# One layer of a hybrid streaming encoder on one core: the output projection's gate summed on VectorE, inverse roots as exp of a logarithm, capped decay differences as Relu

## The chip, the core and the metric

The kernel runs on one core of one Trainium2 chip. The core has five engines with a queue each: PE (TensorE, matmuls), DVE (VectorE), ACT (ScalarE), POOL (GpSimd) and SP (SyncE, which here only issues DMAs). The metric is the device time of one execution in microseconds (us).

## What is computed

One layer for two request groups that share the weights, 256 prompt tokens and 32 sample tokens (together T = 288 columns; 128 features to a partition tile, NB = 16 tiles for 2048). Everything is in fp32. Cut to what matters here:

```python
shift1, scale1, gate1, shift2, scale2, gate2 = split(silu(c) @ w_mod + b_mod, 6)
h = rms_norm(x) * (1 + scale1) + shift1
a, b, c_, gates = split(h @ w_in)
y_a = group_rms_norm(gla(a)) * silu(a_g)
y_b = group_rms_norm(ssd(b) * silu(z))
y_c = u * token_mix(layer_norm(v))
merged = sum_k sigmoid(g_k) * (y_k @ w_branch_k)
x = x + gate1 * (merged @ w_out)
x = x + gate2 * (square(relu(h2 @ w_up)) @ w_down)
```

The recurrence of branch B weighs pairs of positions with exp(min(a_t - a_s, 0)), masked to t >= s; the decay difference is capped at zero before the exp.

## The kernel before, in words

All large products go through `product_group`: a tile of 4 x 256 weight columns (512 KB) is loaded by SP into a ring of six `raw` buffers, ACT casts it to its high half (`whi`, line 443), DVE subtracts to get the low half (`wlo`, line 444), and PE runs 24 matmuls of 288 columns with them (lines 461 to 463: low activations with high weights, high with high, high with low). There are three buffers each of `whi` and `wlo`.

The modulation `silu(c) @ w_mod` has six parts of 2048 outputs. Parts 0 and 1 come first (`mod_stream`). The others follow in the order `MOD_PARTS = (2, 4, 3, 5)`; part 2 is `gate1`, the gate of the output projection. They are a generator, `mods`, that the product loops advance by fractions of a step for each weight tile (`mod_rate`, 0.2 to 0.5). One step is one 512 KB tile `mraw` of `w_mod`, in the same ring of six buffers.

Parts 4, 3 and 5 are summed on DVE (`mod_part_ve`, line 302): a unit is 512 columns, 8 steps; in each step four operations multiply a 128 x 512 piece by a column of `cT` and add it to one of two accumulators `macc` (lines 316 and 318). At the end eight small matmuls against `ones2` sum over partitions, ACT copies the result, PE transposes it once and DVE adds the bias (lines 372 to 385, called through `mod_flush`). Part 2 is summed on PE (`mod_parts`, lines 327 to 356): for each pair of tiles eight matmuls of 256 columns in four column groups, then per half of the part one copy on ACT and two transposes.

The mixers run beside the products. `mixer_c` normalises the eight tiles of v on DVE, transposes them on PE, and `finish_c` (line 1060) multiplies with `wsT` on PE, adds and multiplies on DVE (`yC`, `acc`); `split_y` makes `yhi` on ACT and `ylo` on DVE for the branch's products. `mixer_a` runs for eight heads; each builds `z` operands on DVE and ACT for seven levels, and ends with `inv_rms` (line 721): a matmul with `ones`, Sqrt on ACT, reciprocal on DVE. `mixer_b` (line 869) runs eight times; for each of two heads it forms the capped decay differences on DVE (line 923), takes Exp on ACT (lines 926 and 928) and multiplies with `cb` on DVE. After every fourth `mixer_b` and in `mixer_c` there is one more `inv_rms`.

What order the instructions have on each engine is decided when the kernel is built: a scheduler takes the ready instruction of the highest priority, program order with an offset for loads, weight halves and evacuations (`tc.high_priority`). On the chip every queue then runs in that order.

Of the kernel before, what the change touches and what calls it, by code (L numbers as in the profile page):

```python
# [10 lines left out]
F32 = mybir.dt.float32  # L11
# [6 lines left out]
P = 128  # L18
D = 2048
# [21 lines left out]
def tile_step(ctx, tc, io, outs):  # L41
# [12 lines left out]
    MOD_VE = (4, 3, 5)  # L54
# [6 lines left out]

    MODB = 2
# [264 lines left out]
    def mod_parts(parts):  # L327


        for part in parts:  # L330
            if part in MOD_VE:
                yield from mod_part_ve(part)
                continue
            for half in range(2):
                ps = paux.tile([P, 512], F32, tag="modps", name=nm("modps"), bufs=2)
                c0 = part * D + half * 1024
                held = []
                for k in range(NB):
                    with tc.high_priority(offset=PRIO):
                        raw = wpool.tile([P, 1024], F32, tag=MTAG[0], name=nm("mraw"), bufs=MTAG[1])  # L340
                        nc.sync.dma_start(out=raw, in_=wm[:, k, c0:c0 + 1024])
                    held.append((k, raw))
                    if len(held) == MODB:
                        together([partial(TE.matmul, ps[32 * cg:32 * cg + 32, 0:256], cT[:, k1, :],
                                          r[:, cg * 256:(cg + 1) * 256], start=k < MODB and k1 == k,
                                          stop=k == NB - 1 and k1 == held[0][0])
                                  for k1, r in reversed(held) for cg in range(4)])
                        held = []
                    if k == 1:
                        mod_flush()  # L350
                    yield
                with tc.high_priority(offset=PRIO):
                    sb = wpool.tile([P, 256], F32, tag="modsb", name=nm("modsb"), bufs=1)
                    S.copy(out=sb, in_=ps[:, 0:256])
                mod_tail.append((part * NB + half * 8, 0, ps, sb))
        mod_flush()

    mod_tail = []

    def mod_flush():  # L360

        while mod_tail:
            j, n, ps, sb = mod_tail.pop()
            if n:
                for b in range(n):
                    TE.matmul(ps[:, 2 * b:2 * b + 2], sb[:, b * P:(b + 1) * P], selm, start=True, stop=True)
                V.tensor_tensor(out=mod[:, j:j + n, :],
                                in0=ps[:, 0:2 * n].rearrange("p (b s) -> p b s", s=2),
                                in1=par("b_mod", j, n).unsqueeze(2).to_broadcast([P, n, 2]), op=ALU.add)
            else:  # L370
                nb = 2
                if type(sb) is list:
                    nb = 1
                    acc, sb = sb, wpool.tile([P, 256], F32, tag="modsb", name=nm("modsb"), bufs=1)
                    together([partial(TE.matmul, ps[32 * cg:32 * cg + 32, 0:P], ones2[:, s],
                                      acc[s][:, cg * P:(cg + 1) * P], start=s == 0, stop=s == 1)
                              for s in range(2) for cg in range(4)])
                    S.copy(out=sb[:, 0:P], in_=ps[:, 0:P])
                for b in range(nb):
                    TE.transpose(ps[:, b * P:(b + 1) * P], sb[:, b * P:(b + 1) * P], ident)  # L380
                v = ps[:, 0:nb * P].rearrange("p (b g r) -> p g b r", b=nb, r=32)
                m = mod[:, j:j + 4 * nb, :].rearrange("p (g b) s -> p g b s", b=nb)
                V.tensor_tensor(out=m, in0=v[:, :, :, 0:2], op=ALU.add,
                                in1=par("b_mod", j, 4 * nb).rearrange("p (g b) -> p g b", b=nb).unsqueeze(3)
                                .to_broadcast([P, 4, nb, 2]))
# [4 lines left out]
    mods = chain(mod_stream(boot), mod_parts(MOD_PARTS))  # L390
# [330 lines left out]
    def inv_rms(sq, scale):  # L721

        pq = aux()
        TE.matmul(pq[:, 0:T], ones, sq[:, 0:T], start=True, stop=True)
        r = tt("rms")
        S.activation(out=r[:, 0:T], in_=pq[:, 0:T], func=AF.Sqrt, scale=scale, bias=eps_c)
        V.reciprocal(out=r[:, 0:T], in_=r[:, 0:T])
        return r
# [140 lines left out]
    def mixer_b(j):  # L869
# [45 lines left out]
        for a in range(2):  # L915
# [5 lines left out]
            for o, rows, c, t0, n in ((m[:, 0:P], slice(0, P), 0, 0, P), (m[:, P:SEQ], slice(0, P), 1, P, P),  # L921
                                      (ms[LAST, a], LAST, 2, SEQ, DEC)):
                V.tensor_scalar(out=o, in0=pa[rows, t0:t0 + n], scalar1=tkm[rows, c, 1, hh:hh + 1], scalar2=0.0,
                                op0=ALU.subtract, op1=ALU.min)
            S.activation(out=e2[a * BP:(a + 1) * BP, 0:160], in_=pa[a * BP:(a + 1) * BP, 128:T], func=AF.Exp)
            S.activation(out=m[:, 0:SEQ], in_=m[:, 0:SEQ], func=AF.Exp)
            V.tensor_mul(out=m[:, 0:SEQ], in0=m[:, 0:SEQ], in1=cb[:, 0:SEQ])
        S.activation(out=ms[LAST], in_=ms[LAST], func=AF.Exp)
# [108 lines left out]
    def mixer_c():  # L1037
# [11 lines left out]
        rs = inv_rms(ss, 1.0 / 1024)  # L1049
# [286 lines left out]
```

## Time and profile before

| | us |
|---|---|
| median of 3 runs | 2059.65 (2055.81 to 2063.46) |
| the profiled execution | 2054.64 |
| its span, first to last instruction | 2052.9 |
| mean granted clock of PE in it | 0.993 of full speed |

The rows below come from the profiled execution; its times count from the start of the span. In a row of a group of instructions stand: line, engine, operation, output<-inputs, shapes, count, then busy time, mean ns of one, and the idle time of the engine before them with what ended it. PE's durations overlap, so starts are compared there.

### The profile page before, as it was taken

Reading aid. Unit: us, or ns where it says so; the run is one execution under the profiler, and the core shown is the slowest. Engines: PE = TensorE matmul, PEld = TensorE weight load, DVE = VectorE, ACT = ScalarE, POOL = GpSimd, SP = SyncE. Lnnn points to the kernel's source line nnn. Section 1 sums busy time; section 2 is a strip of 40 time slices with the busy share of each in tenths; the row PEclk is TensorE's granted clock in tenths of the full one; section 3 lists DMA queues with packets and bytes.
Section 4 is the critical chain, followed back from the end, with each engine's and each line's share of the span. In section 5 each row is a group of like instructions: output and inputs, shape, how many; then the busy total and the mean of one; then the engine's idle time right before and its main releaser. Section 6 shows DMA issues by size and latency. Waiting matters only on the chain.

```text
span 2052.9 us, 40220 instructions
## 1 busy us (share of the span) xinstructions
PE 2002.9 (98%) x16248; PEld 1941.6 (95%) x16248; DVE 1450.8 (71%) x2515; ACT 990.9 (48%) x1547; POOL 154.8 (8%) x284
## 2 busy tenths in 40 slices
PE   5999999999999999999999999999999999999997
PEld 3888999989999999999999999999999999999997
DVE  2585767866679878798889998675864455555564
ACT  3432595675555545555344544433443344334443
POOL 3020220100101101011000100000000000000010
PEclk8999999999999999999999999999999999999999
DMA  9998745556576766577777777575655555555542
GB/s 259 312 315 267 224 137 165 176 166 200 184 226 191 212 192 199 174 229 242 226 248 235 228 237 225 185 226 185 218 192 163 162 163 166 168 165 162 167 157 88
DMA packets 364874, 412.29 MB, mean 201 GB/s; under 512 B 14808, under 2 KB 325488, under 8 KB 364688
## 3 DMA queue, kind: packets, MB, share of 16 engines
q1 hardware_dynamic: 360784, 403.97, 63.2%
q0 software_dynamic: 3040, 4.58, 1.0%
q8 instruction: 127, 2.08, 0.4%
q10 hardware_dynamic: 864, 1.18, 0.2%
q14 instruction: 59, 0.48, 0.1%
HBM read 405.05 MB, written 4.62 MB: 200 GB/s over the span
## 4 chain that ended last, share of the span: by engine, by line
PE 61%; DVE 0%; ACT 0%; DMA 0%; issue 0%; DVEq 0%; ACTq 0%
PE mm L463 20%; PE mm L461 20%; PE mm L462 20%; DMA mraw<-in_w_mod_dram 0%; PE aux L1226 0%; PE aux L210 0%; ACT stage L1300 0%; PE aux L897 0%; PE modps L77 0%; PE modps L80 0%; PE aux L80 0%; PE aux L936 0%; DVE macc L318 0%; PE aux L885 0%; DVE wlo L444 0%
## 5 line engine op out<-in xcount | busy, mean ns | idle before, releaser
L443 ACT CAST whi<-raw 128x1024 fp32r<-128x1024 f32 x568 | 595.4, 1049 | 835.9 <-PE mm L462 652.8
L444 DVE TENSOR_TENSOR wlo<-raw,whi 128x1024 fp32r<-128x1024 f32 x568 | 695.2, 1225 | 410.5 <-ACT whi L443 408.8
L461 PE MATMUL mm<-hlo,whi 128*128 128x288 f32 x1408 | 419.8, 299 | 1.2 <-ACT sg L974 1.2
L462 PE MATMUL mm<-hhi,whi 128*128 128x288 f32 x1408 | 417.1, 297 | 0.0
L463 PE MATMUL mm<-hhi,wlo 128*128 128x288 f32 x1408 | 412.3, 297 | 1.7 <-DVE wlo L444 1.7
L461 PE MATMUL mm<-h2lo,whi 128*128 128x290 f32 x1024 | 304.4, 298 | 0.0
L462 PE MATMUL mm<-h2hi,whi 128*128 128x290 f32 x1024 | 303.7, 297 | 0.0
L463 PE MATMUL mm<-uhi,wlo 128*128 128x288 f32 x1024 | 303.2, 296 | 0.0
L463 PE MATMUL mm<-h2hi,wlo 128*128 128x290 f32 x1024 | 301.8, 297 | 0.0
L462 PE MATMUL mm<-uhi,whi 128*128 128x288 f32 x1024 | 301.3, 294 | 0.0
L461 PE MATMUL mm<-ulo,whi 128*128 128x288 f32 x1024 | 301.0, 294 | 0.0
L318 DVE SCALAR_TENSOR_TENSOR macc<-mraw,cT,macc 128x512 f32<-128x512 f32 x360 | 261.3, 754 | 29.8 <-DMA mraw<-in_w_mod_dram 29.6
L461 PEld LDWEIGHTS mm<-hlo,whi 128*128 128x128 f32 x1408 | 265.5, 189 | 4.7 <-issue 2.2
L463 PEld LDWEIGHTS mm<-hhi,wlo 128*128 128x128 f32 x1408 | 263.2, 189 | 3.7 <-DVE wlo L444 2.6
L462 PEld LDWEIGHTS mm<-hhi,whi 128*128 128x128 f32 x1408 | 265.9, 189 | 0.5
L463 PEld LDWEIGHTS mm<-h2hi,wlo 128*128 128x128 f32 x1024 | 194.3, 190 | 0.3 <-issue 0.2
L462 PEld LDWEIGHTS mm<-h2hi,whi 128*128 128x128 f32 x1024 | 194.5, 190 | 0.0
L461 PEld LDWEIGHTS mm<-h2lo,whi 128*128 128x128 f32 x1024 | 193.6, 189 | 0.5 <-issue 0.4
L461 PEld LDWEIGHTS mm<-ulo,whi 128*128 128x128 f32 x1024 | 193.0, 188 | 0.4 <-issue 0.4
L462 PEld LDWEIGHTS mm<-uhi,whi 128*128 128x128 f32 x1024 | 192.4, 188 | 0.0
L463 PEld LDWEIGHTS mm<-uhi,wlo 128*128 128x128 f32 x1024 | 192.2, 188 | 0.1
L430 PE MATMUL mm<-hlo,whi 128*128 128x288 f32 x448 | 136.8, 306 | 0.4 <-DVE hlo L530 0.4
(421 smaller groups left out, 3079.8 us busy)
## 6 DMA issues: line engine op xcount, KB each, us to landing
raw<-in_w_in_dram SPq DMA_DIRECT2D x204, 512.0 KB, 4.4
mraw<-in_w_mod_dram SPq DMA_DIRECT2D x128, 512.0 KB, 4.3
raw<-in_w_up_dram SPq DMA_DIRECT2D x128, 512.0 KB, 3.8
raw<-in_w_down_dram SPq DMA_DIRECT2D x128, 512.0 KB, 3.5
raw<-in_w_mod_dram SPq DMA_DIRECT2D x64, 512.0 KB, 5.9
raw<-in_w_branch_dram SPq DMA_DIRECT2D x48, 512.0 KB, 4.5
raw<-in_w_out_dram SPq DMA_DIRECT2D x32, 512.0 KB, 4.7
raw<-in_w_in_dram SPq DMA_DIRECT2D x56, 256.0 KB, 5.1
```

Source lines behind the costliest of these rows:

```text
L318: V.scalar_tensor_tensor(out=acc[s], in0=raw[:, i], scalar=cs, in1=acc[s], op0=ALU.mult, op1=ALU.add)
L430: TE.matmul(pt, whi[:, i, cs], alo[k], start=i == 0, stop=False)
L443: S.copy(out=whi, in_=raw)
L444: V.tensor_sub(out=wlo, in0=raw, in1=whi)
L461: TE.matmul(pts[b], whi[:, i, cs], alo[k], start=k == 0, stop=False)
L462: TE.matmul(pts[b], whi[:, i, cs], ahi[k], start=False, stop=False)
L463: TE.matmul(pts[b], wlo[:, i, cs], ahi[k], start=False, stop=k == nk - 1)
```

## The change

Three edits. First, part 2 of the modulation goes the way of parts 4, 3 and 5, through `mod_part_ve`; `mod_parts` and the special cases in `mod_flush` go. Second, `inv_rms` takes exp(-0.5 ln(v)) on ACT in place of Sqrt on ACT and reciprocal on DVE, for the eight heads of `mixer_a` and the two groups of `mixer_b`; `mixer_c` keeps the old form. Third, the capped difference of `mixer_b` becomes Relu(a_s - a_t) on ACT, and the Exp behind it takes the scale -1.

```diff
-    def mod_parts(parts):
-        for part in parts:
-            if part in MOD_VE:
-                yield from mod_part_ve(part)
-                continue
-            for half in range(2):
-                ps = paux.tile([P, 512], F32, tag="modps", name=nm("modps"), bufs=2)
...
-                    if len(held) == MODB:
-                        together([partial(TE.matmul, ps[32 * cg:32 * cg + 32, 0:256], cT[:, k1, :],
-                                          r[:, cg * 256:(cg + 1) * 256], start=k < MODB and k1 == k,
-                                          stop=k == NB - 1 and k1 == held[0][0])
-                                  for k1, r in reversed(held) for cg in range(4)])
...
@@ mod_flush
-                nb = 2
-                if type(sb) is list:
-                    nb = 1
-                    acc, sb = sb, wpool.tile([P, 256], F32, tag="modsb", name=nm("modsb"), bufs=1)
-                    together([partial(TE.matmul, ps[32 * cg:32 * cg + 32, 0:P], ones2[:, s],
-                                      acc[s][:, cg * P:(cg + 1) * P], start=s == 0, stop=s == 1)
-                              for s in range(2) for cg in range(4)])
-                    S.copy(out=sb[:, 0:P], in_=ps[:, 0:P])
-                for b in range(nb):
-                    TE.transpose(ps[:, b * P:(b + 1) * P], sb[:, b * P:(b + 1) * P], ident)
...
+                sums, sb = sb, wpool.tile([P, P], F32, tag="modsb", name=nm("modsb"), bufs=1, padded_shape=[P, 512])
+                together([partial(TE.matmul, ps[32 * cg:32 * cg + 32, 0:P], ones2[:, s],
+                                  sums[s][:, cg * P:(cg + 1) * P], start=s == 0, stop=s == 1)
+                          for s in range(2) for cg in range(4)])
+                S.copy(out=sb, in_=ps[:, 0:P])
+                TE.transpose(ps[:, 0:P], sb, ident)
...
-    mods = chain(mod_stream(boot), mod_parts(MOD_PARTS))
+    mods = chain(mod_stream(boot), *[mod_part_ve(part) for part in MOD_PARTS])
@@ inv_rms
-    def inv_rms(sq, scale):
+    def inv_rms(sq, scale, root=False):
...
-        S.activation(out=r[:, 0:T], in_=pq[:, 0:T], func=AF.Sqrt, scale=scale, bias=eps_c)
-        V.reciprocal(out=r[:, 0:T], in_=r[:, 0:T])
+        if root:
+            S.activation(out=r[:, 0:T], in_=pq[:, 0:T], func=AF.Sqrt, scale=scale, bias=eps_c)
+            V.reciprocal(out=r[:, 0:T], in_=r[:, 0:T])
+        else:
+            S.activation(out=r[:, 0:T], in_=pq[:, 0:T], func=AF.Ln, scale=scale, bias=eps_c)
+            S.activation(out=r[:, 0:T], in_=r[:, 0:T], func=AF.Exp, scale=-0.5)
@@ mixer_b
-                V.tensor_scalar(out=o, in0=pa[rows, t0:t0 + n], scalar1=tkm[rows, c, 1, hh:hh + 1], scalar2=0.0,
-                                op0=ALU.subtract, op1=ALU.min)
+                S.activation(out=o, in_=pa[rows, t0:t0 + n], func=AF.Relu, scale=-1.0, bias=tkm[rows, c, 1, hh:hh + 1])
             S.activation(out=e2[a * BP:(a + 1) * BP, 0:160], in_=pa[a * BP:(a + 1) * BP, 128:T], func=AF.Exp)
-            S.activation(out=m[:, 0:SEQ], in_=m[:, 0:SEQ], func=AF.Exp)
+            S.activation(out=m[:, 0:SEQ], in_=m[:, 0:SEQ], func=AF.Exp, scale=-1.0)
             V.tensor_mul(out=m[:, 0:SEQ], in0=m[:, 0:SEQ], in1=cb[:, 0:SEQ])
-        S.activation(out=ms[LAST], in_=ms[LAST], func=AF.Exp)
+        S.activation(out=ms[LAST], in_=ms[LAST], func=AF.Exp, scale=-1.0)
@@ mixer_c
-        rs = inv_rms(ss, 1.0 / 1024)
+        rs = inv_rms(ss, 1.0 / 1024, True)
```

The scheduler then gives other orders. Line numbers of the changed kernel are about 40 lower. Three places follow. The first is PE's queue where branch C begins, the first product with a mixer's result (`mm<-ylo`). Before (`L1064` is the token product of `finish_c`, `L77` and `L80` the gate's matmuls):

```order
L1064 MATMUL aux_3372<-wsT,vtC_3303 128x128 x2
L1064 MATMUL aux_3372<-wsTs,vtC_3303 128x32
L462 MATMUL mm_3862<-hhi_2399,whi_3965 128x288
L463 MATMUL mm_3862<-hhi_2399,wlo_3966 128x288
L77 MATMUL modps_2327<-mraw_4537,cT 32x256
L80 MATMUL modps_2327<-mraw_4537,cT 32x256 x3
L80 MATMUL modps_2327<-mraw_4437,cT 32x256 x4
L1064 MATMUL aux_3380<-wsT,vtC_3312 128x128 x2
L1064 MATMUL aux_3380<-wsTs,vtC_3312 128x32
L461 MATMUL mm_4375<-ylo_4344,whi_4379 128x288
```

The same place after the change (`L555` is the last transpose of mixer C's v, `L1026` the token product of `finish_c`):

```order
L555 MATMUL aux_3363<-ident,acc_285 128x128 x3
L1026 MATMUL aux_3369<-wsT,vtC_3299 128x128 x2
L1026 MATMUL aux_3369<-wsTs,vtC_3299 128x32
L1026 MATMUL aux_3377<-wsT,vtC_3308 128x128 x2
L1026 MATMUL aux_3377<-wsTs,vtC_3308 128x32
L1026 MATMUL aux_3385<-wsT,vtC_3317 128x128 x2
L1026 MATMUL aux_3385<-wsTs,vtC_3317 128x32
L1026 MATMUL aux_3393<-wsT,vtC_3326 128x128 x2
L1026 MATMUL aux_3393<-wsTs,vtC_3326 128x32
L1026 MATMUL aux_3401<-wsT,vtC_3335 128x128 x2
L1026 MATMUL aux_3401<-wsTs,vtC_3335 128x32
L420 MATMUL mm_4376<-ylo_4345,whi_4380 128x288
```

Three finishes had product matmuls around them before the first `ylo`; now five stand in a row behind the last transpose, and the gate's matmuls are gone.

The second place is DVE's queue between mixer C's normalisation and its first `yC` (`L444` and `L403` are the low weight halves). Before:

```order
L444 TENSOR_TENSOR wlo_3966<-raw_3963,whi_3965 128x1024
L444 TENSOR_TENSOR wlo_4380<-raw_4377,whi_4379 128x1024
L444 TENSOR_TENSOR wlo_4410<-raw_4407,whi_4409 128x1024
L1066 TENSOR_TENSOR yC_3368<-aux_3364,bsb 128x256
L1069 TENSOR_TENSOR yC_3368<-aux_3364,bsb 128x32
```

After the change the gate's sums (`L313`, `L315`) stand between the halves; eight of them come before the first `yC`, the start of which is:

```order
L403 TENSOR_TENSOR wlo_3967<-raw_3964,whi_3966 128x1024
L403 TENSOR_TENSOR wlo_4381<-raw_4378,whi_4380 128x1024
L313 TENSOR_SCALAR macc_4439<-mraw_4441,cT 128x512
L313 TENSOR_SCALAR macc_4440<-mraw_4441,cT 128x512
L315 SCALAR_TENSOR_TENSOR macc_4439<-mraw_4441,cT,macc_4439 128x512
L315 SCALAR_TENSOR_TENSOR macc_4440<-mraw_4441,cT,macc_4440 128x512
L403 TENSOR_TENSOR wlo_4411<-raw_4408,whi_4410 128x1024
L315 SCALAR_TENSOR_TENSOR macc_4439<-mraw_4545,cT,macc_4439 128x512
```

Four more lie further on, between the `yC` and `ylo` operations: 12 in all between the normalisation and the last `ylo` of the branch.

The third place is ACT's queue at an inverse root of mixer A. Before, a table load and Sqrt (`L726`), then the load for the next Exp:

```order
L726 ACT_TABLE_LOAD
L726 ACTIVATE rms_4165<-aux_4163,eps_c 128x288
L630 ACT_TABLE_LOAD
L630 ACTIVATE z_4174<-z_4174 128x288
L684 ACTIVATE eb_4298<-bA_3583 128x160
```

After, Ln (`L689`) and Exp (`L690`), each with a load of its own at this root:

```order
L689 ACT_TABLE_LOAD
L689 ACTIVATE rms_4339<-aux_4337,eps_c 128x288
L690 ACT_TABLE_LOAD
L690 ACTIVATE rms_4339<-rms_4339 128x288
L402 CAST whi_5597<-raw_5595 128x1024
```

At some of the other roots no load stands ahead of Ln or of Exp; the ten roots have 12 loads on these two lines, and ACT has 84 loads in all where it had 82.

## Rows read from the trace of the kernel before

**Rows 1.** The page's busy time, share of the span and instructions of PE and DVE
```profile
PE 2002.9 (98%) x16248; PEld 1941.6 (95%) x16248; DVE 1450.8 (71%) x2515; ACT 990.9 (48%) x1547; POOL 154.8 (8%) x284
```

**Rows 2.** Windows: stretch, length, busy of PE, PEld, DVE, ACT, POOL; PEclk, DMA, GB/s
```profile
206.00:590.00 384.00, 375.27 (x3568) 357.37 (x3568) 272.69 (x595) 245.91 (x393) 51.46 (x98) 0.99 0.60 182
590.00:660.00 70.00, 69.75 (x716) 68.51 (x717) 66.79 (x148) 46.19 (x78) 8.28 (x12) 1.00 0.66 206
660.00:970.00 310.00, 306.66 (x2439) 301.45 (x2438) 264.83 (x455) 164.26 (x262) 37.92 (x77) 1.00 0.67 206
```

**Rows 3.** Waits of PE, 206 to 590 us: total us, times, longest
```profile
PE aux L77 <- DVE z L632: 2.9, 1, 2.9
PE aux L596 <- ACT vA L598: 2.7, 1, 2.7
PE aux L77 <- DVE ddt L821: 1.8, 1, 1.8
```

**Rows 4.** Windows with the end of the first two of these waits
```profile
354.00:358.00 4.00, 3.37 (x80) 3.33 (x81) 3.94 (x17) 0.94 (x4) 0.00 (x0) 0.58 0.46 137
416.00:420.00 4.00, 3.19 (x15) 3.19 (x16) 1.90 (x8) 3.97 (x8) 0.00 (x0) 0.57 0.46 131
```

**Rows 5.** Timeline of PE at one group of part 2's matmuls: start, us, instruction
```profile
585.03 0.29 PE L463 MATMUL mm<-hhi,wlo 128*128 128x288 f32 x1
585.25 0.40 PE L77 MATMUL modps<-mraw,cT 128*32 128x256 f32 x1
...
586.25 0.40 PE L461 MATMUL mm<-hlo,whi 128*128 128x288 f32 x1
586.49 0.29 PE L462 MATMUL mm<-hhi,whi 128*128 128x288 f32 x1
```

**Rows 6.** Timeline of PE at the closing matmuls and the transpose of a unit
```profile
1534.42 0.30 PE L462 MATMUL mm<-uhi,whi 128*128 128x288 f32 x1
1534.55 0.29 PE L463 MATMUL mm<-uhi,wlo 128*128 128x288 f32 x1
...
1535.59 0.29 PE L462 MATMUL mm<-uhi,whi 128*128 128x288 f32 x1
...
1538.49 0.30 PE L463 MATMUL mm<-uhi,wlo 128*128 128x288 f32 x1
...
1538.86 0.30 PE L462 MATMUL mm<-uhi,whi 128*128 128x288 f32 x1
```

**Rows 7.** Groups of DVE's instructions by line and form, whole span
```profile
L318 DVE SCALAR_TENSOR_TENSOR macc<-mraw,cT,macc 128x512 f32<-128x512 f32 x360 | 261.3, 754 | 29.8 <-DMA mraw<-in_w_mod_dram 29.6
L727 DVE RECIPROCAL rms<-rms 128x288 f32<-128x288 f32 x11 | 21.4, 1949 | 3.1 <-ACT rms L726 3.1
L316 DVE TENSOR_SCALAR macc<-mraw,cT 128x512 f32<-128x512 f32 x24 | 10.9, 484 | 8.8 <-DMA mraw<-in_w_mod_dram 4.7 <-PE modps L80 4.0
L923 DVE TENSOR_SCALAR m<-aux,tkm 128x128 f32<-128x128 f32 x32 | 9.7, 345 | 3.8 <-PE aux L918 3.7
L923 DVE TENSOR_SCALAR mpad<-aux,tkm 32x32 f32<-32x32 f32 x16 | 4.1, 259 | 0.5
```

**Rows 8.** Timeline of DVE, two sums back to back
```profile
613.84 1.41 DVE L318 SCALAR_TENSOR_TENSOR macc<-mraw,cT,macc 128x512 f32<-128x512 f32 x2
```

**Rows 9.** Window from mixer C's reciprocal to the start of branch C
```profile
309.00:338.00 29.00, 29.00 (x243) 27.51 (x242) 19.14 (x33) 15.23 (x24) 4.42 (x9) 1.00 0.60 188
```

**Rows 10.** Longest of PE's waits, 660 to 1232 us
```profile
PE mm L463 <- DVE wlo L444: 1.7, 2, 1.1
```

**Rows 11.** Groups of ACT's instructions by line and form, whole span
```profile
L726 ACT ACT_TABLE_LOAD x11 | 14.1, 1283 | 0.2
L689 ACT ACTIVATE kd<-bA 128x128 f32<-128x128 f32 x16 | 5.6, 395 | 1.6 <-PE aux L80 1.5
L574 ACT ACTIVATE az<-az 128x288 f32<-128x288 f32 x8 | 3.3, 438 | 0.0
```

**Rows 12.** Waits of SP's queue, 590 to 1232 us
```profile
SPq L450 <- DVE macc L318: 52.9, 33, 5.0
```

More of the change, by code (lines that the diff above doesn't have):

```diff
@@ L53, in tile_step @@
     MOD_PARTS = (2, 4, 3, 5)
-    MOD_VE = (4, 3, 5)
     MODR, RS, RA, RB, RD, RW, RC = 1.5, 0.2, 0.4, 0.3, 0.5, 0.5, 0.25
@@ L60, in tile_step @@
     MTAG = ("raw", RAW)
-    MODB = 2
     EVB = 6
@@ L325, in mod_part_ve @@
         mod_flush()
-    def mod_parts(parts):
-        for part in parts:
-            if part in MOD_VE:
-                yield from mod_part_ve(part)
-                continue
-            for half in range(2):
-                ps = paux.tile([P, 512], F32, tag="modps", name=nm("modps"), bufs=2)
[L336 to L342, printed above, removed]
-                    if len(held) == MODB:
-                        together([partial(TE.matmul, ps[32 * cg:32 * cg + 32, 0:256], cT[:, k1, :],
-                                          r[:, cg * 256:(cg + 1) * 256], start=k < MODB and k1 == k,
-                                          stop=k == NB - 1 and k1 == held[0][0])
-                                  for k1, r in reversed(held) for cg in range(4)])
[L348 to L356, printed above, removed]
     mod_tail = []
@@ L370, in mod_flush @@
             else:
-                nb = 2
-                if type(sb) is list:
-                    nb = 1
-                    acc, sb = sb, wpool.tile([P, 256], F32, tag="modsb", name=nm("modsb"), bufs=1)
-                    together([partial(TE.matmul, ps[32 * cg:32 * cg + 32, 0:P], ones2[:, s],
-                                      acc[s][:, cg * P:(cg + 1) * P], start=s == 0, stop=s == 1)
-                              for s in range(2) for cg in range(4)])
-                    S.copy(out=sb[:, 0:P], in_=ps[:, 0:P])
-                for b in range(nb):
-                    TE.transpose(ps[:, b * P:(b + 1) * P], sb[:, b * P:(b + 1) * P], ident)
[L381 to L385, printed above, removed]
+                sums, sb = sb, wpool.tile([P, P], F32, tag="modsb", name=nm("modsb"), bufs=1, padded_shape=[P, 512])
[4 more added lines that the diff above has]
+                TE.transpose(ps[:, 0:P], sb, ident)
+                V.tensor_tensor(out=mod[:, j:j + 4, :], in0=ps[:, 0:P].rearrange("p (g r) -> p g r", r=32)[:, :, 0:2],
+                                in1=par("b_mod", j, 4).unsqueeze(2).to_broadcast([P, 4, 2]), op=ALU.add)
     KG = ((0, 2), (2, 2), (4, 2), (6, 2), (8, 4), (12, 4))
     boot = [(part * D + k0 * P, nk * P) for k0, nk in KG for part in (0, 1)]
-    mods = chain(mod_stream(boot), mod_parts(MOD_PARTS))
+    mods = chain(mod_stream(boot), *[mod_part_ve(part) for part in MOD_PARTS])
     mod_count = [0]
```

## The prediction

> **What bounds the kernel now.** I read the page's busy table first. TensorE (PE) is busy for 98% of the span and VectorE (DVE) for 71% [rows 1], so a change pays only where it takes instructions or waits off PE, and hurts wherever PE is made to wait. The average hides the stages, so the next view is the busy time of the stretches [rows 2]. The one this change works on is 206 to 590 us: here part 2 of the modulation (the output projection's gate) is computed in 32 steps, one 512 KB tile each, beside mixer C and six of the eight heads of mixer A. PE is busy for 375.27 of 384 us, so it idles 8.7 us; DVE for 272.69 us, 71%. Behind it the gates that DVE already sums run beside mixers too: from 590 to 660 us DVE is 95.4% busy (66.79 of 70 us) and PE idles 0.25 us; from 660 to 970 us, 85% and 3.3 us. Then the waits of PE in the first stretch [rows 3]: three single waits, 2.9 us on DVE, 2.7 us on ACT and 1.8 us on DVE. In the two windows with the end of the first two the granted clock is 0.58 and 0.57 [rows 4], so PE worked there partly at 1.2 GHz.
>
> **What PE loses and gains.** The removed matmuls run four at a time in column groups, so the durations of their rows must not be added. I take starts instead. Two product matmuls with a group of eight gate matmuls between them start 585.03 and 586.49, 1.46 us apart [rows 5], where neighbours without a group start 0.13 us apart (1534.42 and 1534.55 [rows 6]), or 0.27 for the two steps: one group costs 1.19 us. Part 2 has 32 tiles and one group for two tiles, so 16 groups, 19.0 us, and four transposes at 0.10 us (0.37 us between the starts around one, less 0.27 [rows 6]), 0.4 us. Added are four units of the DVE form, each with eight matmuls against the ones (1.04 us between the starts around them, less 0.27: 0.77 [rows 6]) and one transpose: 4 x 0.87 = 3.5 us. Net **15.9 us less on PE**, all in a stretch where PE sets the pace.
>
> **What DVE gains and loses.** Each of the 32 steps becomes four operations of 128 x 512. 120 of them are scalar_tensor_tensor at 754 ns [rows 7]; back to back, two take 1.41 us [rows 8], so one then adds 0.66 us. Eight are the first of a sum, a tensor_scalar at 484 ns [rows 7], 0.40 with the same overlap. That is 82 to 94 us. Off DVE go six of the reciprocals of mixer A at 1949 ns [rows 7] in this stretch, 11.7 us (mixer C keeps its own). So DVE needs 272.7 + (82 to 94) - 11.7 = 343 to 355 us, while PE, if it idles as now, would be through in 384 - 15.9 = 368 us: a DVE share of 93 to 96.5%. The nearest row is 590 to 660 us, which holds 95.4% with the same mixture and leaves PE alone. So DVE just fits, with no slack for a late operation.
>
> **Where it does not fit smoothly.** The order of PE at the start of branch C shows it: five finishes of mixer C now stand in one block ahead of the first branch matmul, with no product matmul between them, where they were spread before. DVE has 12 of the new operations ahead of the last ylo of that branch. Eight come between weight halves, and there DVE has room: 19.14 of 29 us busy from 309 to 338 us [rows 9]. Four lie inside the chain yC, ylo that PE waits for, 2.7 us. Bounds for this place: the 2.9 us wait that is there now and its half clock may vanish (4.6 us gained), or all 12 operations may reach PE (8 us lost). I take 3 us lost, near the four operations in the chain. For the rest of the stretch I take 1 us more of waiting for wlo: from 660 to 1232 us, at 85% and more of DVE, PE waits 1.7 us for it [rows 10]. Its bounds are -4.5 us (the ACT wait of 2.7 us and the 1.8 us wait vanish) and +8 us (PE waits each time DVE falls a tile behind).
>
> The clock belongs to these waits. Two of the three above were followed by work at half clock; such a piece costs about 1.7 us (4 us at 0.57 of the clock [rows 4] is 4 x 0.43). I count no more and no fewer of them than now. The Trainium skill, TensorE: Matmul & The Clock Gate, section "HAM oscillation — how this bites in real kernels", speaks against a change that trades PE work for waits: gaps in PE's work throttle it, and the work behind starts cold. The trace agrees for two waits and not for the 1.8 us one. By that rule taken for every new wait, three new ones would cost 5 us more and the sum would be some 7 us faster instead of 12.
>
> **Edits with one answer.** The decay differences take 32 operations of 345 ns and 16 of 259 ns off DVE [rows 7], 15 us by their means, and put as many Relu on ACT, 19 us at most (kd, of the larger size and with a bias too, is 395 ns [rows 11]). They lie in 660 to 970 us, where ACT is 53% busy and PE waits 3.3 us in all, so this is worth 0, between a gain of 3.3 us and a loss of 3. The inverse roots lose Sqrt and reciprocal and gain Ln and an Exp of 438 ns [rows 11], ten times; the table load stays, and the order has 12 loads at the ten roots, since Ln and Exp of one root can each need their own, and 84 loads in all for 82. At 1283 ns [rows 11] that is 2.6 us more of ACT, which is 64% busy in the first stretch. Nothing on PE waits for a root within its mixer; the products that use it come later. If that cover were gone, a root would be shorter, not longer: 1.95 us of reciprocal against 0.44 of Exp and at most one load of 1.28. Cost 0. The DMA tiles stay at 512 KB and keep their places in SP's order; a tile is now held until DVE is through with it, instead of until its pair has arrived and PE has run.
>
> **The sum.** -15.9 + 3 + 1 = -11.9 us, **12 us faster**. The profiled execution took 2054.64 us (span 2052.9), so 2042.6 on its scale; the median of the runs shown is 2059.65, 5.0 us higher, and on that scale the prediction is **2047.5 us**. Half a per cent, about what a measurement here can tell from no change, is 10.3 us.
>
> **Rivals.**
> *The whole gain and the old waits too.* The waits of rows 3 come from an order that is now another. If mixer A's shorter DVE chain removes two of them with their half clock, 15.9 + 6 = 22 us are gained: 2037.5. For it: 590 to 660 us runs at 95.4% of DVE with PE full. Against it: the packed block at branch C.
> *DVE becomes the bound.* If DVE, with its own waits on PE and ACT, is busy for only 92.5% of the stretch, 355 us of work take the old 384 us and nothing is gained; 94% gives 378 us, 91% 390. I give it -6 to +6 us, 2059.5 in the middle. For it: mixer A's short dependent operations come in bursts, and six heads lie here where the 95.4% row has one or two. Against it: that row, and that PE's idle 8.7 us now are not DVE's doing alone. The point is the forecast's own length, 372 us: it needs 92 to 95.4% of DVE, the upper end just what the row holds.
> *Slower: gate tiles hold up the weights.* SP's queue is in order and gates and weights share six raw buffers. Behind 590 us the weights' DMA waits for macc 33 times, 52.9 us, 1.6 us each [rows 12]. 32 new steps could add 51 us of such waiting; if half reaches PE, 26 us, the gain is turned into a loss of 10 us: about 2070. It decides where gate tiles fill half the ring while DVE is behind. Against it: behind 590 us such waits hardly reach PE.
> *The change not doing what it says* touches only the roots: two loads instead of none saved, 2.6 us of ACT off the path.
>
> **How the numbers follow.** Forecast (7 to 17 us faster, 2042.5 to 2052.5) 0.50; the whole gain 0.17; DVE bound 0.26; slower 0.07. About two thirds of the forecast's band lies beyond 10.3 us: faster 0.17 + 0.34 = 0.51; same 0.16 + 0.26 = 0.42; slower 0.07. The range leaves out the slower case, the end of the whole gain beyond 22.5 us and the DVE case beyond +1.4 us, together 0.2: 2037 to 2061.
>
> **What would show it.** Right: no gate matmul of 256 columns; PE busy down by about 16 us; in the stretch that holds part 2, DVE at 93 to 97% and some 12 us of PE idle, most of it where branch C begins; macc at about 0.75 us; PE waits in 660 to 1232 us about as now. Wrong: PE idle there of 20 us or more with waits on wlo or z (DVE bound), ACT's whi waiting for weight DMAs (the held-up ring), or idle under 5 us (the whole gain).

## The result, and the profile after

The change is **slower**: 2072.28 us against 2057.2, six runs each; ratio 1.006, interval 1.0047 to 1.0073, so some 12 us. The profiled execution took 2074.52 us with a span of 2072.7.

The page's busy line of the changed kernel:

```profile
PE 1999.2 (96%) x16056; PEld 1944.7 (94%) x16056; DVE 1500.8 (72%) x2587; ACT 1009.5 (49%) x1609; POOL 155.4 (7%) x284
```

PE has 192 instructions fewer than in [rows 1] and is busy only 3.7 us less. The windows of the changed kernel, columns as in [rows 2]:

```profile
206.00:590.00 384.00, 360.39 (x3313) 348.37 (x3312) 332.74 (x701) 230.41 (x381) 51.40 (x95) 0.98 0.60 179
590.00:660.00 70.00, 70.00 (x646) 68.94 (x645) 63.12 (x125) 42.30 (x67) 5.38 (x15) 1.00 0.71 216
660.00:970.00 310.00, 298.56 (x2401) 293.85 (x2401) 238.21 (x409) 190.15 (x331) 31.13 (x68) 0.98 0.63 191
970.00:1232.00 262.00, 262.00 (x2045) 259.84 (x2044) 244.70 (x396) 123.27 (x191) 27.38 (x23) 1.00 0.78 240
```

Against [rows 2] PE's idle time is 23.6 us for 8.7 from 206 to 590 us, and 11.4 for 3.3 from 660 to 970. DVE is busy for 332.74 of 384 us, 87% and not 93 to 97. Where the time goes shows if both kernels are compared at the same product matmul, counted from the start. The changed one is 7.1 us behind at the 1200th (247 us in the kernel before), 4.0 ahead at the 2500th (480 us), 7.8 behind at the 3500th (634 us), 10.6 at the 4500th (788 us) and 21.0 at the 5600th (949 us). Behind 970 us both run alike, and it stays some 20 us behind to the end.

PE's waits in the changed kernel, the longest from 206 to 660 us, then those from 660 to 970, which is mixer B's stretch (total us, times, longest):

```profile
PE mm L420 <- ACT whi L402: 4.9, 1, 4.9
PE mm L422 <- DVE wlo L403: 3.5, 5, 1.2
PE mm L420 <- ACT iv L563: 2.5, 1, 2.5
PE aux L1026 <- DVE yC L1031: 2.3, 2, 1.5
PE aux L74 <- DVE z L591: 1.7, 2, 1.1
...
PE aux L74 <- DVE mpad L891: 8.1, 4, 3.9
PE aux L870 <- DVE stB L867: 2.6, 1, 2.6
PE mm L422 <- DVE wlo L403: 0.7, 1, 0.7
```

The long waits of [rows 3] are gone or shorter, and new ones stand at other places: all listed waits from 206 to 660 us come to 23.3 us (8.8 before), those from 660 to 970 to 11.4 (3.3 before). Behind six of these places PE worked at 1.2 GHz; windows of the changed kernel over the first and the last of these pieces, and the sum of the six:

```profile
283.80:290.60 6.80, 4.70 (x18) 4.42 (x19) 4.10 (x6) 6.74 (x10) 0.00 (x0) 0.50 0.27 77
...
894.80:898.20 3.40, 3.40 (x17) 3.39 (x16) 3.37 (x8) 0.20 (x1) 0.00 (x0) 0.50 0.52 154
sum 27.20, PE 23.39 PEld 22.83 DVE 22.64 ACT 15.22 POOL 1.67; mean PE 3.90 PEld 3.81 DVE 3.77 ACT 2.54 POOL 0.28
```

Behind 206 us the kernel before has two such windows, 6.6 us with 5.99 of PE work. Half of the work time in them is lost: 11.7 against 3.0 us. (It has one more ahead of 206 us, where PE waits for DMA in both kernels; at the 900th product matmul, 204 us, they are 1.2 us apart.) The profiled spans differ by 19.8 us. PE's idle time in the whole span grew by 23.5 us, from 50.0 to 73.5, and 22.6 of that are the listed waits; its busy time fell by 3.7, which is some 12.4 us less work and 8.7 more lost to the clock. By the medians the difference is less, 15.1 us: the profiled execution of before lies 2.6 us below its median, that of the change 2.2 above.

Three places show how the waits come about. **The dt matmuls.** The 48 small matmuls for dt, the step sizes of branch B's recurrence, which no line of the diff touches, stand earlier in PE's order. Windows of the instructions that touch the high half of their weights (32 of the 48 matmuls), PE's time behind the length, of before and then of the change:

```profile
206.00:250.00 44.00, 0.00 (x0) 0.00 (x0) 0.42 (x1) 0.41 (x1) 1.00 0.76 231
262.00:275.00 13.00, 5.94 (x30) 2.83 (x30) 0.00 (x0) 0.00 (x0) 1.00 0.45 138
```

```profile
206.00:250.00 44.00, 5.92 (x28) 2.66 (x28) 0.42 (x1) 0.40 (x1) 1.00 0.70 216
262.00:275.00 13.00, 0.84 (x4) 0.38 (x4) 0.00 (x0) 0.00 (x0) 1.00 0.42 120
```

A little later ACT has one table load after another and starts no weight half for 9 us. Timeline of ACT in the changed kernel:

```profile
275.72 1.03 ACT L402 CAST whi<-raw 128x1024 fp32r<-128x1024 f32 x1
...
277.48 1.28 ACT L733 ACT_TABLE_LOAD   x1
...
279.67 1.28 ACT L926 ACT_TABLE_LOAD   x1
...
281.42 1.28 ACT L776 ACT_TABLE_LOAD   x1
...
283.18 1.28 ACT L777 ACT_TABLE_LOAD   x1
...
284.82 1.03 ACT L402 CAST whi<-raw 128x1024 fp32r<-128x1024 f32 x1
```

The kernel before has the same hole (halves at 270.3 and 279.5 us), but there the dt matmuls were PE's work until 272.6 us, so that it came to the hole with weights in hand. In the change 42 of the 48 are done some 35 us earlier and PE runs dry: the 4.9 us wait, with half clock behind it. What this place is worth in the end is another matter (e9, e18 and e17 below). The other two places are read below, where an edit stands alone.

### The profile page after: what moved, and what is told of

It is laid out like the page before. It is cut to its first block, busy times and chain, and to the rows that moved or that the text cites. A ratio compares the mean times of both kernels' runs of the same rounds, so it can differ in the third digit from the quotient of the medians.

```text
span 2072.7 us, 40003 instructions
## 1 busy us (share of the span) xinstructions
PE 1999.2 (96%) x16056; PEld 1944.7 (94%) x16056; DVE 1500.8 (72%) x2587; ACT 1009.5 (49%) x1609; POOL 155.4 (7%) x284
## 4 chain that ended last, share of the span: by engine, by line
PE 83%; DVE 6%; DMA 5%; ACT 3%; issue 2%; POOL 0%; ACTq 0%; SPq 0%; DVEq 0%; POOLq 0%
PE mm L422 24%; PE mm L420 24%; PE mm L421 24%; DMA mraw<-in_w_mod_dram 2%; PE mm L389 2%; PE mm L391 2%; PE mm L390 2%; DVE wlo L403 2%; DVE macc L315 2%; DMA raw<-in_w_mod_dram 1%; PE modps L74 1%; ACT whi L402 1%; PE aux L77 1%; PE modps L77 1%; DMA xt<-in_x_prompt_dram 0%
## 5 line engine op out<-in xcount | busy, mean ns | idle before, releaser
L403 DVE TENSOR_TENSOR wlo<-raw,whi 128x1024 fp32r<-128x1024 f32 x568 | 696.1, 1227 | 370.6 <-ACT whi L402 364.4
L315 DVE SCALAR_TENSOR_TENSOR macc<-mraw,cT,macc 128x512 f32<-128x512 f32 x480 | 346.3, 753 | 45.8 <-DMA mraw<-in_w_mod_dram 45.3
```

The source lines that it names most:

```text
L315: V.scalar_tensor_tensor(out=acc[s], in0=raw[:, i], scalar=cs, in1=acc[s], op0=ALU.mult, op1=ALU.add)
L403: V.tensor_sub(out=wlo, in0=raw, in1=whi)
```

## Experiments

Ratios are to the kernel before, run beside each. One per mille is 2 us.

**Each edit alone.** e1: the hunks on `mod_parts`, `mod_flush` and `mods` of the diff, nothing else:

```diff
-    mods = chain(mod_stream(boot), mod_parts(MOD_PARTS))
+    mods = chain(mod_stream(boot), *[mod_part_ve(part) for part in MOD_PARTS])
```

> Only part 2 of the modulation is moved from PE to DVE; roots and decay differences as before. Theory W (waits): PE's busy time falls by about 16 us as predicted, but PE idles about 20 us more between 206 and 660 us and runs some pieces at half clock, so this edit alone is worth between -4 and +10 us. Rival B (the decay differences do the damage): this edit alone gives the predicted gain, 10 to 16 us faster, and the loss comes with the Relu. Rival L (any other order of the instructions shifts the time by as much): no number for it; the kernel with another order and the same work, sent beside it, tells.

1.0034 (1.0021 to 1.0047): 7 us slower. Rival B falls, the gate alone loses. Its DVE is busy for 49.10 us from 450 to 500 and 37.96 from 550 to 590, so locally full. What that does, in the timelines of this kernel (DVE; then ACT and PE; `sp` and `kA` are operands of a head of mixer A, `iv` is the copy of a product that frees its accumulator):

```profile
506.43 1.41 DVE L315 SCALAR_TENSOR_TENSOR macc<-mraw,cT,macc 128x512 f32<-128x512 f32 x2
507.87 0.46 DVE L536 SCALAR_TENSOR_TENSOR sp<-mm,l 128x288 f32<-128x288 f32 x1
```

```profile
508.37 0.53 ACT L544 ACTIVATE kA<-sp,lbt 128x288 f32<-128x288 f32 x1 [4.25 <-DVE sp L536]
509.03 0.70 ACT L563 COPY iv<-mm 128x288 f32<-128x288 f32 x2
...
509.48 0.41 PE L420 MATMUL mm<-hlo,whi 128*128 128x288 f32 x1 [3.69 <-ACT iv L563]
```

From 503.28 to 507.84 four gate sums, 2.8 us in all, and shorter operations stand ahead of the short sp; ACT stands 4.25 us idle for sp with iv queued behind it, and PE waits 3.69 us for iv. DVE's order, not its mean share, made this wait. In the change the same wait is 2.5 us.

e2: only the decay differences.

```diff
-                V.tensor_scalar(out=o, in0=pa[rows, t0:t0 + n], scalar1=tkm[rows, c, 1, hh:hh + 1], scalar2=0.0,
-                                op0=ALU.subtract, op1=ALU.min)
+                S.activation(out=o, in_=pa[rows, t0:t0 + n], func=AF.Relu, scale=-1.0, bias=tkm[rows, c, 1, hh:hh + 1])
```

> Only the 48 decay differences are moved from DVE to ACT. Theory W: PE's waits for the masked products (mpad) in mixer B, 660 to 970 us, rise by 6 to 8 us and one to three half-clock pieces of 1.7 us come with them: 8 to 12 us slower; the stretch up to 660 us stays as it is. Rival B2 (mixer B lost its time to the roots' table loads, not to the Relu): within 3 us of before. The forecast's own step was 0, within 3 us.

1.0039 (1.0026 to 1.0053): 8 us slower, at mpad, the decay masks of the sample tokens, as expected, with 6.8 us at 0.50 behind the longest wait:

```profile
PE aux L77 <- DVE mpad L928: 9.1, 4, 4.4
```

The kernel before has 0.7 us there. The timeline of ACT in e2 at one head pair:

```profile
844.88 1.28 ACT L924 ACT_TABLE_LOAD   x1
846.17 0.30 ACT L924 ACTIVATE e<-aux 64x160 f32<-64x160 f32 x1
846.49 1.28 ACT L973 ACT_TABLE_LOAD   x1
847.78 0.41 ACT L973 ACTIVATE sg<-mm 128x288 f32<-128x288 f32 x1
848.21 1.28 ACT L925 ACT_TABLE_LOAD   x1
849.51 0.42 ACT L925 ACTIVATE m<-m 128x256 f32<-128x256 f32 x1
...
850.88 1.28 ACT L973 ACT_TABLE_LOAD   x1
...
853.43 1.28 ACT L924 ACT_TABLE_LOAD   x1
...
855.48 0.25 ACT L927 ACTIVATE mpad<-mpad 32x64 f32<-32x64 f32 x1
```

and the same Exp in the kernel before:

```profile
847.47 1.28 ACT L926 ACT_TABLE_LOAD   x1
848.77 0.42 ACT L926 ACTIVATE m<-m 128x256 f32<-128x256 f32 x1
...
851.15 0.25 ACT L928 ACTIVATE mpad<-mpad 32x64 f32<-32x64 f32 x1
```

In e2 sigmoids of a merge gate (L973) fell between a head's Exp: five loads and 10.9 us until the masks are done, where one load and 3.9 us stood. From a pair's first decay matmul to its finished mask the 5th to 7th pair take 12.9, 11.9 and 12.1 us for 7.8, 8.0 and 9.9, and PE, which had the mask 2.2 to 2.5 us in hand there, now waits for it.

e3: only the inverse roots; the Sqrt form stays for mixer C.

```diff
-        S.activation(out=r[:, 0:T], in_=pq[:, 0:T], func=AF.Sqrt, scale=scale, bias=eps_c)
-        V.reciprocal(out=r[:, 0:T], in_=r[:, 0:T])
+            S.activation(out=r[:, 0:T], in_=pq[:, 0:T], func=AF.Ln, scale=scale, bias=eps_c)
+            S.activation(out=r[:, 0:T], in_=r[:, 0:T], func=AF.Exp, scale=-0.5)
```

> Only the ten inverse roots are changed (Ln and Exp on ACT for Sqrt and reciprocal). Theory W: nothing waits for a root, within 3 us of before, and DVE is busy for some 19.5 us less. Rival B2: the table loads delay mixer B's exponentials, 5 to 10 us slower with PE's new waits in 660 to 970 us.

0.9979 (0.9969 to 0.9989): 4 us faster, and DVE is busy for 1434.2 us, 16.6 less. The 2.7 us wait of PE for ACT in [rows 3] is gone from this order; where the rest comes from the profile does not show (its profiled execution is 1.6 us longer than that of the kernel before). The three edits alone add up to +5.2 per mille, near the +6.0 of the change.

e4: the same instructions in another order.

```diff
-    EVP = 1500
+    EVP = 1300
```

> The kernel before with the same instructions in another order (the priority that evictions get is 1300 in place of 1500; some two thousand places of PE's order move). Theory W: the time is set by work and by the waits of the chains, which stay: within 5 us of before. Rival L: the order alone moves the time by 8 us or more in either direction, and then a difference of 12 us says little of the three edits.

0.9993 (0.9983 to 1.0003): same. This one other order keeps the three waits of [rows 3]. It shows that a new order need not matter, and no more: e10 and e15 below are the same instructions in two orders, and they differ by 11 per mille.

**What in the gate edit costs.** e5: e1 with short sums in part 2; the other columns of the gate are left out.

```diff
+                        w = 128 if part == 2 else 512
-                            V.scalar_tensor_tensor(out=acc[s], in0=raw[:, i], scalar=cs, in1=acc[s],
+                            V.scalar_tensor_tensor(out=acc[s][:, 0:w], in0=raw[:, i, 0:w], scalar=cs,
+                                                   in1=acc[s][:, 0:w], op0=ALU.mult, op1=ALU.add)
```

> The gate on DVE as in the run with that edit alone, but each of its sums reaches over 128 of the 512 columns of a tile (the other columns of the gate are left out); DMA tiles, their places in the queue and PE's work stay as they are there. Theory C (DVE's time in the chains: the sums stand in DVE's order between the short dependent operations of mixer A, and each pair of them adds 1.4 us to what PE waits for): with about 60 us less of DVE work from 206 to 660 us PE's idle time there falls from about 25 us to 10 to 14 us, and the kernel is 8 to 16 us faster than before. Rival D (the tiles' DMA: DVE waits for a gate tile, or the tiles hold up the weights): within 6 us of the run with full sums, 3 to 10 us slower than before. Rival A (ACT's new order around the dt chain, seven table loads close together): the 4.9 us wait at 284 us stays and with it part of the loss: 0 to 8 us faster.

0.9969 (0.9961 to 0.9978): 6 us faster, 13 better than e1. The time lies below theory C's 8 to 16 us, in the range of theory A. From 206 to 660 us PE idles for 18.0 us, where e1 has 27.2 and theory C expected 10 to 14. The windows of e1 and e5:

```profile
206.00:590.00 384.00, 358.03 (x3224) 345.14 (x3225) 335.67 (x687) 244.27 (x387) 47.45 (x88) 0.98 0.58 175
```

```profile
206.00:590.00 384.00, 366.04 (x3377) 356.62 (x3376) 303.08 (x712) 256.47 (x401) 52.88 (x98) 0.98 0.60 182
```

So DVE's time is the larger part of what the gate edit lost against its forecast, but not all. SP's queue waits for the sums for 64.7 us in 34 waits from 206 to 970 us, where e1 has 40.5 in 21, so the ring of gate tiles does not explain these 13 us. A 4.3 us wait at the dt chain (for its last operand, ddt) stayed.

e7: the change without the Relu.

> The change without the Relu: gate on DVE and the new inverse roots. If the three edits add up (gate alone 7.3 us slower, roots alone 4.4 us faster, Relu alone 8 us slower, the change 12 us slower): 3 us slower than before, between -1 and +7. If the roots pay more where DVE is full, because six reciprocals of 1.95 us leave mixer A's stretch: 0 to 8 us faster. If mixer B's loss in the whole change is not the Relu's: 8 us slower or more.

1.0013 (1.0003 to 1.0022): 3 us slower; the edits add up.

e8: e7 with gate steps moved from mixer A to mixer B.

```diff
-    MODR, RS, RA, RB, RD, RW, RC = 1.5, 0.2, 0.4, 0.3, 0.5, 0.5, 0.25
+    MODR, RS, RA, RB, RD, RW, RC = 1.5, 0.2, 0.2, 0.45, 0.5, 0.5, 0.25
```

> The change without the Relu and with the gate steps spread otherwise: 0.2 steps per weight half in mixer A in place of 0.4, 0.45 in mixer B in place of 0.3; all are done by the same time. Theory C (the sums cost by where they stand, in mixer A's chains with DVE above 93 per cent): PE idles 6 to 12 us less from 206 to 660 us, and the kernel is 4 to 12 us faster than the same kernel with the old rates, so 1 to 9 us faster than before. Rival M (mixer B's chains suffer as much): within 3 us of the run with the old rates, the idle time moved to 660 to 970 us.

0.9965 (0.9953 to 0.9977): 7 us faster than before, 10 better than e7. From 206 to 590 us 80 gate sums stand where the change has 122. The windows of e7 and e8:

```profile
206.00:590.00 384.00, 360.15 (x3316) 348.65 (x3315) 333.39 (x702) 230.89 (x382) 53.20 (x95) 0.98 0.60 179
```

```profile
206.00:590.00 384.00, 371.29 (x3413) 362.33 (x3414) 314.60 (x671) 241.19 (x399) 51.96 (x98) 0.99 0.57 170
```

From 206 to 660 us PE idles for 13.8 us, where e7 has 23.9: theory C.

e9 and e10: the dt matmuls held behind the last product of the first product stage, in e1 and in e8.

```diff
+        with tc.issue_after(lastmm[0].ins):
-        for k in range(NB):
+            for k in range(NB):
```

> The gate on DVE alone, as in the run with that edit alone, but the 48 small dt matmuls (6.4 us of PE) are held behind the last product of the first product stage, where the kernel before has them; in that run 42 of the 48 had moved 35 us earlier. Theory H (they covered the 8 to 9 us in which ACT, with one table load after another, hands over no weight half): PE's 4.9 us wait at 289 us and its 6.8 us at half clock vanish or fall to the 1.8 us that the kernel before has: 4 to 8 us faster than the run with the gate edit alone, 0 to 3 us slower than before. Rival: the wait only moves, to where the weights are late next: within 2 us of the run with the gate edit alone.

> Gate and roots with the gate steps spread, as in the run before, and the dt matmuls held as well. Theory H: the gain of the two repairs adds up, 4 to 8 us faster than the spread kernel, 11 to 16 us faster than before, near the 12 us that were forecast. Rival: within 2 us of the spread kernel.

e9 1.0024 (1.0012 to 1.0035), 2 us better than e1 with intervals that overlap; e10 0.9939 (0.9919 to 0.9959), 13 us faster than before. In both the 4.9 us wait for whi became one of 3.5 us for ddt. In e9 that is mostly the rival, the wait moves. e10 is 5 us better than e8, as theory H had it, but the intervals overlap and the runs are of different sets, and e16 and e17 below differ only in this hold and do not show the gain again.

e11 and e15: e10 with still fewer steps in mixer A (0.1 and 0.5; 0.15 and 0.4).

> As the kernel with the spread steps and the dt matmuls held, but with only 0.1 gate steps per weight half in mixer A and 0.5 in mixer B. Theory C (a DVE that is 93 per cent busy in a mixer delays the chains): mixer A's waits fall further, by 1 to 3 us, and mixer B, now above 93 per cent, gives back more: 0 to 6 us slower than with the milder spread. Rival M0 (only mixer A's chains are tender): 1 to 4 us faster than it.

> Gate and roots, dt matmuls held, 0.15 gate steps per weight half in mixer A and 0.4 in mixer B. Theory C (only the load in mixer A's chains counts, and e11 lost its gain at the end of mixer B, where 0.5 steps leave DVE no room): within 4 us of the kernel with 0.2 and 0.45, 8 to 16 us faster than before. Rival L (each place of the steps deals new waits at random): anywhere between 14 us faster and 8 us slower than before, with new waits at new places.

e11 1.0018 (1.0002 to 1.0034), e15 1.0053 (1.0036 to 1.0071): worse, and each in one place. At the 5200th product matmul they are 18 and 12 us ahead of the kernel before. Then PE's waits, e11 at 994 to 1001 us, e15 at 1209 to 1216:

```profile
PE aux L685 <- POOL ssB L915: 4.5, 1, 4.5
PE aux L215 <- DMA xs<-in_x_sample_dram: 3.2, 1, 3.2
```

```profile
PE mm L422 <- ACT whi L404: 7.3, 2, 5.8
PE aux L1168 <- DVE rst L1140: 5.5, 1, 5.5
```

e11 meets DVE with the end of mixer B and the steps together (297.74 of 310 us busy there), e15 at the end of the output projection, where DVE is busy for 28.56 of 32 us. Theory C's size was wrong for both. Rival L is not refuted here: each loss has its place at a hand-over of stages, but I could not have told which beforehand, and e15 came out slower than even L's range. That 0.2 and 0.45 do well over the whole kernel is therefore in part a lucky choice of two numbers.

What all runs agree on is the stretch itself. At the 3500th product matmul (634 us in the kernel before) the five kernels with the full sums at the old rates (the change, e1, e7, e9, e18) are 7.3 to 17.9 us behind the kernel before, e5 with its short sums 0.9 behind, and the six with fewer sums there (e8, e10, e11, e15, e16, e17) 5.6 to 11.2 ahead. The seven runs with the gate still on PE (e2, e3, e4, e6, e12, e13, e14) lie between 0.1 ahead and 6.0 behind.

**What in the Relu edit costs.** e6: all Relu of a pair first, then its Exp with a higher priority than the sigmoids. e12: the whole chain of a head with that priority.

```diff
+        with tc.high_priority(offset=EVP + 200):
```

> The decay differences as Relu on ACT, as in the run with that edit alone, but both heads' Relu are written first and then all their Exp, with a higher priority than the merge gates' sigmoids, so that fewer of those come between a head's Exp. Theory T (the loss in mixer B is ACT's table loads between Relu and the two Exp of a head, in the chain that PE's masked products wait for): ACT's table loads fall by three and PE's waits for mpad from about 9 us to under 4 us: within 4 us of before. Rival R (the Relu themselves, 48 operations of 0.3 to 0.4 us in ACT's order, make the chain longer): 6 to 11 us slower than before, as with that edit alone.

> The decay differences as Relu on ACT alone, and the whole chain of a head (the decay's matmul, Relu and Exp) gets a higher priority than the merge gates' sigmoids and the evictions. Theory R (the Relu come late because they stand behind the other work in ACT's order, and DVE's product of the mask stands behind them): PE's waits for mpad fall from 9 us to under 4 us, within 4 us of before. Rival (ACT's longer chain itself, whatever stands before it): 5 to 9 us slower than before, as with the edit alone.

1.0034 (1.0017 to 1.005) and 1.0028 (1.0015 to 1.004): not repaired. Waits for mpad stay (7.0 us in e6, 5.4 in e12), and some pairs still need 11 to 14 us. e6 has three table loads fewer than e2, as expected, and hardly gains by it. By themselves these speak for ACT's longer chain: theory R in e6, the rival in e12.

e13 and e14: the sigmoids of the second branch held on ACT behind the pairs' last Exp, with and without the Relu.

```diff
+            with tc.issue_after(lastexp[0].ins) if kk == 0 else nullcontext():
+                S.activation(out=sg[j], in_=ps, func=AF.Sigmoid)
```

> The decay differences as Relu on ACT alone, with the sigmoids of the second branch's merge gate held on ACT behind the last Exp of the two heads before them; ACT's table loads fall from 89 to 73. Theory T (the switches make the chain late): PE's waits for mpad under 4 us, and within 3 us of the same kernel without the Relu (the next run). Theory R (the Relu's own time): 5 to 9 us slower than the next run.

> The kernel before with the same sigmoids held in the same way, and no other edit; table loads 73 in place of 82. It is the base for the run with the Relu. The held sigmoids can delay the branch's evictions: between 5 us faster and 10 us slower than before.

1.0304 (1.029 to 1.0317) and 1.029 (1.0275 to 1.0306). With equal switches the Relu cost 3 us or nothing. But both kernels are some 60 us slower than before, far outside what was expected for e14, with waits at new places (mpad 19.3 us in e14, sigmoids 18.2 in e13), so this pair is inconclusive.

e16 and e17 settle more: e10 with the Relu, and the whole change with nothing but e8's two numbers.

> The kernel with the spread gate steps and the dt matmuls held, and the Relu on ACT as well. If the Relu's loss is a matter of ACT's order in mixer B, it is there again: 5 to 10 us slower than without them, with 6 us and more of PE's waits for mpad. If the 15 us that DVE is spared pay where it is 92 per cent busy: 0 to 4 us faster than without them.

> The whole change (gate, roots, Relu) with only the two numbers altered: 0.2 gate steps per weight half in mixer A, 0.45 in mixer B. If the places of the gate steps are the cause: 8 to 14 us faster than before, with PE's waits for mpad under 2 us, since mixer B's order is another with them. If the Relu's loss stands on its own: 0 to 4 us faster than before, with the mpad waits of 8 us there.

0.9931 (0.9919 to 0.9943) and **0.9919 (0.9903 to 0.9934): the change with two other numbers is 17 us faster than before**, faster than both kernels of this case and than the 8 to 14 us expected. e16 is level with e10: the Relu neither cost nor gave anything there. The kernel before was not run with the two numbers, so how much of the 17 us they would give without the three edits is open. Windows of e17:

```profile
206.00:590.00 384.00, 371.72 (x3417) 362.53 (x3416) 313.65 (x669) 241.19 (x398) 51.41 (x98) 0.99 0.57 170
590.00:660.00 70.00, 68.95 (x742) 67.62 (x741) 58.75 (x139) 42.23 (x72) 4.39 (x12) 1.00 0.56 169
660.00:970.00 310.00, 310.00 (x2454) 305.10 (x2452) 276.44 (x451) 189.29 (x327) 44.65 (x79) 1.00 0.74 229
```

From 660 to 970 us ACT does the same 189 us of work as in the change, all Relu included, and PE never waits. The 5th to 7th pair have their masks after 8.6, 7.7 and 7.5 us. On the lines of mixer B's Exp ACT has 9 table loads there in place of 13. So the Relu's own time on ACT does not cost 8 us; the order that they and the other work fall into does. That the table loads are the part of this order that counts is likely from the timeline of e2, but no run shows it by itself. Against e8, the same without the Relu, e17 is even 9 us better (0.9919 to 0.9965): there DVE was busy for 285.75 of those 310 us, here for 276.44. Between e10 and e16 the same step gives 2 us, which is within the noise.

e18: the change with the dt matmuls held alone.

> The whole change with the old numbers and only the dt matmuls held. As with the gate alone the 4.9 us wait turns into a shorter one for ddt: 1 to 4 us faster than the change, 8 to 11 us slower than before. If the held matmuls are what the repaired kernel lives on: 5 us or more faster than before.

1.0055 (1.0039 to 1.0071): no gain over the change. At the 1200th product matmul e18 is 1.4 us behind the kernel before, where the change is 7.1 behind; at the 2000th it is 4.2 for 4.8, so what the hold gives is lost again within 150 us. e17 keeps the 4.9 us wait and is the fastest kernel. The two numbers carry the repair.

## Why the prediction was wrong, point by point

- **PE's work, -15.9 us: right in size, as far as runs show.** In the kernel before each of the 16 groups takes 1.22 to 1.23 us from the start ahead of it to the start behind it, like the one of [rows 5]. By busy time, with the clock's loss behind 206 us taken off, PE's work fell by 12.4 us in the change. In e17, whose half-clock windows come to 10.2 us (6.6 before), PE is busy for 1990.1 us, 12.8 less than [rows 1], and its work fell by some 14. Such sums hold to a few us: in e4 the instructions of the kernel before are busy 2.2 us longer. The sums cost 753 ns each, as [rows 7] said.
- **"So DVE just fits, with no slack for a late operation" and "3 us lost" plus "1 us more of waiting": this step failed.** PE waits 14.5 us more from 206 to 660 us, not 4, with DVE at 87%, less than the 93 to 96.5% that were to fit. I checked the mean share of DVE against a row where the same mixture fits, and looked at one place, the start of branch C (there 2.3 and 0.9 us of waits; 3 taken). The sums cost at places I did not look at, among them the one in front of sp in mixer A. The sign that I gave for this, 20 us and more of idle time, came (23.6), but wlo and z, the waits that I named with it, make up only 6.5 of the 23.3 us listed. e5 gives 13 us back for shorter sums, e8 10 for fewer sums there.
- **The order of PE moved where the diff has nothing.** The dt matmuls left a hole in ACT's hand-over uncovered, 4.9 us and its half clock. I had not asked what hides ACT's holes in the old order, neither for the matmuls that I took away nor for those that moved in their place. This step was missing, but it is not what made the change slower: with the old rates, holding the matmuls gave 1 to 2 us, within the noise (e9, e18).
- **"I count no more and no fewer of them than now": failed.** There are six pieces at 1.2 GHz for two, 8.7 us. The rule of the Trainium skill, TensorE: Matmul & The Clock Gate, section "HAM oscillation — how this bites in real kernels", that gaps throttle PE and the work behind starts cold, agrees with the trace for these six; I had weighed it as 5 us and not taken it.
- **Decay differences "worth 0, between a gain of 3.3 us and a loss of 3": outside on the first order.** Alone they cost 8 us (e2). ACT's 53% share said nothing of the chain from the decay matmul to mpad, in which other work of ACT, with table loads of its own, can stand. With other rates they cost nothing (e16) or gain (e17).
- **Inverse roots "Cost 0": 4 us faster** (e3), by waits that the profile does not show. DVE's relief of 16.6 us was taken as worth nothing without a check of what stands behind it.
- **The rivals.** "DVE becomes the bound" is nearest in cause, but by 87% of DVE, below the 91% that it named, and not by the share. "Gate tiles hold up the weights" gave the nearest time (2070), but by luck: in e5 the ring is waited for no less than in e1, and 13 us come back.

## What to carry to other kernels

A busy share that fits says nothing of the places: before long operations go to another engine, walk the short dependent chains on that engine and count what will stand in front of each link. Work that hides another engine's hole is part of a kernel's order; after a change, list what moved on PE though no line of it was edited. And when work changes engine, tune the rates that place it again before judging the change: here the same edits were 12 us slower or 17 us faster by two numbers. Try several, and run the old kernel with them too, which was left undone here: of the three new pairs of rates tried, two only moved the loss to a later stage (e11, e15).

## What was not expected of the hardware

In the changed kernel each of its five waits of 2.4 to 4.9 us, and one group of three shorter ones, had work at 0.50 of the clock behind it; in e11 three waits of 4.5, 3.2 and 1.3 us within 8 us had a piece of 13.7 us with them. But the same wait went either way: the 2.7 us one of [rows 3] had half clock behind it in the kernel before and none in e6 and e12, the 1.8 us one had none in the kernel before and 3.4 us in e3.
